# Hybrid decoder step: the first GLA tile's gate behind the sampled chunks, scaling inside their folds, and the mixed rows' loads and high parts in another order

## The chip, the cores and the metric

The kernel runs on one core of a Trainium2 chip. TensorE (PE) multiplies matrices into PSUM banks; VectorE (DVE), ScalarE (ACT) and GpSimd (POOL) work on SBUF and PSUM; SyncE (SP) issues nearly all transfers, one after another. Each engine goes through its own instructions in order, and waits where an operand is not there. The metric is the device time in microseconds of one execution.

## What is computed

One layer of a decoder for 2048 prompt rows and 64 sampled rows (8 sequences of 8), width 1024, in float32:

```python
h = rms_norm(x, g_mix_pre)
proj = jnp.einsum('btd,de->bte', h, w_in)
q, k, v, gq, gk, gv, gr, glr = jnp.split(proj, points, axis=-1)
# group A: sliding-window attention with sinks on q, k, v
# group B: gated linear attention, 4 heads, dk 64, dv 128
log_a = log_sigmoid(glr @ w_gk2 + b_gk) / 16
o, s_new = gla_chunked(gq, gk, gv, log_a, s_init)
o = rms_norm(o, g_gla) * silu(gr)
mix = jnp.concatenate([attn, gla_out], -1) @ w_out
x = x + rms_norm(mix, g_mix_post)
# then x + rms_norm(relu(rms_norm(x) @ w_up) ** 2 @ w_down)
```

Since the norm before the projection is one factor for a row (`rstd`), the kernel projects the unscaled rows and multiplies the result by `rstd` when it leaves PSUM.

## The kernel before

Matrix products run in a TensorE format of fewer bits, so each operand is split into a high and a low part, and three products (high-high, high-low, low-high) make one. The 2048 prompt rows are 16 tiles of 128 rows; the 64 sampled rows are a 17th, number 16 (`NB`).

The program has stages. In the first, attention (group A) runs, and the transposed rows go to DRAM. In the second, which the change touches and which lies at about 305 to 680 us of the profile, the gated linear attention goes through the 16 tiles in order (`gla(i)`, a generator), while TensorE fills the gaps between its small products with projections. This second stream, `fill`, is made by `products`: for the sampled rows, and then for tiles 2 to 15, four chunks of 384 columns each (`projecting`), and after the last chunk the output projection (`out_projecting`) of the first two mixed tiles, 0 and 4. The tables `G_FIRST_FILL`, `G_FILL` and `G_LAST_FILL` say how many products of `fill` TensorE does at each `yield` of `gla(i)`; nothing else sets the order, and ScalarE, VectorE and SP do their parts in the order in which the program is written (`InOrder`, whose line 143 the profile names for nearly all of them).

A chunk's products go into one of two PSUM banks of the kind `a`. A chunk of a prompt tile is copied out by ScalarE, times `rstd`. The sampled rows have 64 rows alone, so their low parts are laid beside the high ones: one product of 128 rows gives both halves. Then `folded` has ScalarE copy the lower 64 rows of the bank to `gp_s` and VectorE add the upper 64, and a second ScalarE copy multiplies by `rstd`. Only after VectorE's addition may TensorE use the bank again, for the chunk after next.

In `gla(i)`: level sums of the log decays of 16 to 64 rows, weighted keys and queries (`XK`, `XQ`), the decays of the next tile, the gate (`gate`: four passes of ScalarE and two products over `sg`), the first level sums of the next tile, the queries and keys of the next tile turned by VectorE (`turn`, through `blocks` and DRAM `qk_d`); then TensorE's level products (`gl`, `gh`, `ds`), VectorE's masked copies of them to `AH`, the copies to `AT`, and, some twenty `fill` products later, the products `o` with `AT`. The steps for the sampled rows (`gla_sample`) lie between those of the tiles from tile 1 on.

At the end of the stage, with tile 15 (the last of `fill`), the weights of a done chunk give their place to the output weights `wo`, which had been split and stored to DRAM before (`wo_d`), and to the mixed rows of tiles 0 and 4:

```python
if after is None:
    load_wo(ks, c)
    if c == G_ORDER[1]:
        placed = [place_mix(j) for j in B_ORDER[:2]]
```

`load_wo` puts `k` = 0 to 2 in the place of chunk 1, 3 to 5 in that of chunk 2, 6 and 7 in that of chunk 3, the first 512 columns first; `place_mix` loads the raw rows to `mt` in the place of chunk 0; `split_mix` with `apart` makes their high parts on ScalarE at once and puts their low parts on the list `lows`, from which `gla(15)` takes them.

Of the kernel before, what the change touches and what calls it, by code (L numbers as in the profile page):

```python
# [16 lines left out]
ALU = mybir.AluOpType  # L17
# [57 lines left out]
G_ORDER = (0, 1, 2, 3)  # L75
G_FILL = (3, 5, 6, 10, 8, 2, 14, 4, 4, 10, 8, 20)
G_LAST_FILL = (2, 4, 5, 7, 6, 2, 11, 2, 3, 7, 6, 15)
G_FIRST_FILL = (6, 6, 6, 10, 10, 4)
S_WAIT = (2, 6)
WO_PARTS = ((), (0, 1, 2), (3, 4, 5), (6, 7))  # L80
B_ORDER = (*(j + b for j in range(4) for b in (0, 4)), NB, *(j + b for j in range(4) for b in (8, 12)))
# [72 lines left out]
def hybrid_step_kernel(ctx: ExitStack, tc: tile.TileContext, I, O):  # L154
# [481 lines left out]
    def projecting(i, xT, chunks, act=nc.scalar):  # L636

        n, waiting = rows(i), []
        for c in chunks:
            p_ = bank([P, 512], "a", f"gproj_{i}_{c}")  # L640
            _, wh, wl = gw[c]
            products = ((xT[1], wh), (xT[1], wl)) if i == NB else ((xT[0], wh), (xT[0], wl), (xT[1], wh))
            for k in range(KT):
                for u, (x, w) in enumerate(products):
                    te.matmul(
                        p_[:, :G_N], x[:, k, :], w[:, k, :],
                        start=k + u == 0, stop=k == KT - 1 and u == len(products) - 1,
                    )
                    yield
                    if waiting and (k, u) == (0, 2):  # L650
                        act.activation(*waiting.pop(), scale=rstd_all[:n, i : i + 1])
            if i not in gps:
                gps[i] = gp_pool.tile([P, G_W], F32, tag="gp", name=f"gp_{i}", bufs=2)
            out = gps[i][:n, c * G_N : (c + 1) * G_N]
            src = folded(out, p_[:, :G_N], act, dv) if i == NB else p_[:, :G_N]
            if act is ac and (i, c) == (0, chunks[0]):
                waiting.append((out, src, AF.Copy))
            else:
                act.activation(out, src, AF.Copy, scale=rstd_all[:n, i : i + 1])
            projected.add((i, c))  # L660

    def load_cache(name, c):
# [408 lines left out]
    s_oT = ss.tile([P, 4, NS], F32, name="s_oT")  # L1071
    s_sg = ss.tile([NS, 512], F32, name="s_sg")
    s_kx = s_work[:NS].rearrange("p (b k) -> p b k", b=DB)
    nc.gpsimd.memset(next(afters), 0.0)
    for u in range(2):
        nc.vector.memset(S[u], 0.0)
# [206 lines left out]
    def gla(i, gp, og=iter(())):  # L1283
# [3 lines left out]
        assert {(i, 0), (i, 1)} <= projected  # L1287
        before, after = pre.pop(i)
        ends = i in (0, NB - 1)
        fills = iter(G_LAST_FILL if i == NB - 1 else G_FILL if i else G_FIRST_FILL + G_FILL[6:])  # L1290
        if ends:
            qkTs_of[i] = next(qkTs)
            qk_T(i, gp, P, "c")
# [44 lines left out]
        weighted_queries(XQ, dec, qz, 6, LEVELS[6], dv)  # L1338
        yield next(fills) + 2 * (i == 1), False
        next(following, None)  # L1340
        sg = next(sgs)
        gating = gate(i, gp, P, sg)
        yield next(fills), True
# [2 lines left out]
        deque(following, 0)  # L1346
        sums = first_sums(*pre[i + 1], dec) if i < NB - 1 else iter(())
        next(sums, None)
        if i + 1 < NB - 1:
            assert {(i + 1, 0), (i + 1, 1)} <= projected  # L1350
            turn(i + 1, gps[i + 1])
        qd = next(qds)
# [43 lines left out]
                        )  # L1396
        for l, gm in enumerate(levels):
            put_level(AH, gm, msk[:, l], LEVELS[l])
        for g in range(2):
            ac.activation(AT[:HD, 2 * g : 2 * g + 2, HD:], far[half_of[g]], AF.Copy)  # L1400
        put[:] = [dv.tensor_copy(AT[half_of[1], :, half_of[1]], AH[half_of[1]])]
# [109 lines left out]
    def split_mix(i, m, ks, raw, apart=False):  # L1511
        n = rows(i)
        if apart:
            hi, lo = m[:, 1], m[:, 2]
            ac.activation(hi, raw, AF.Copy)
            for k in range(0, KT, 4):
                kk = slice(k, k + 4)
                lows.insert(
                    len(lows) if k else len(lows) // 2,
                    lambda kk=kk: dv.tensor_tensor(lo[:, kk], raw[:, kk], f32(hi[:, kk]), op=ALU.subtract),  # L1520
                )
            return [[m[:, u, k, :n] for k in range(ks)] for u in (1, 2)]
        if i == NB:
            split_copy(m[:, 1, :, :NS], m[:, 1, :, NS:], raw[:, :, :NS])
            return m[:, 1], None
        split_copy(m[:, 1, :ks, :n], m[:, 2, :ks, :n], raw[:, :ks, :n])
        parts = [[m[:, u, k, :n] for k in range(ks)] for u in (1, 2)]
        if i == NB - 1:
            for t, late in zip(parts, late_mix):
                t.extend(late[:, h, :] for h in range(4))  # L1530
        return parts
# [76 lines left out]
    def products():  # L1608

        xT = {G_NEXT[0]: first_xT}  # L1610
        for i, after in zip(G_NEXT, (*G_NEXT[1:], None)):
# [6 lines left out]
            for c, ks in zip(G_ORDER, WO_PARTS):  # L1618
# [4 lines left out]
                yield from columns  # L1623
                if after is None:
                    load_wo(ks, c)
                    if c == G_ORDER[1]:
                        placed = [place_mix(j) for j in B_ORDER[:2]]
                    if c == G_ORDER[3]:
                        load_wo_half(range(KT), 1)
                        for h, t in enumerate(g_mix):  # L1630
                            sq.dma_start(t, gain_d[h : h + 1].rearrange("a d -> (a d)").partition_broadcast(P))
                        raw = ss.tile([P, KT, P], F32, tag="part1", name="mt_raw", bufs=2)
                        i = B_ORDER[2]
                        sq.dma_start(raw, mix_d[i])
# [39 lines left out]
    wo, pre, ogs_of, mixes, late_mix, g_mix, put, placing, x1_first = {}, {}, {}, {}, [], [], [], [], []  # L1674
    wo_parts = iter(())
    first_xT = load_T(G_NEXT[0], x_place(G_NEXT[0]), sq)
    early, x_loads, put_off, lows, out_stage = [], [], [], [], []

    def take(waiting, n=None):
        for _ in range(len(waiting) if n is None else min(n, len(waiting))):  # L1680
            waiting.pop(0)()
# [912 lines left out]
```

## Time and profile before

| what | value |
|---|---|
| median of 3 runs | 2158.43 us (2155.21 to 2159.4) |
| profiled execution | 2157.64 us, of which the span of its instructions is 2155.9 us |
| TensorE busy | 2135.3 us, 99% of the span |
| VectorE, ScalarE, GpSimd busy | 1521.8, 1220.1, 242.3 us |
| granted TensorE clock, mean | 0.997 |

A row of the timeline gives the start and the length of an instruction or of some equal ones in us, its engine, line and operation, what it writes and reads, and in brackets how long the engine stood idle before it and what ended that. A row of the windows gives a stretch, its length, the busy time of PE, PEld (weight loads), DVE, ACT and POOL with their instructions, the granted clock as a share of full speed, the share of the DMA engines that were busy, and GB/s. A row of the waits gives who waited for whom: us in total, times, longest. A row of the groups gives the line, the engine, the operation, what it writes and reads, shapes and count, then the busy time and the mean in ns, then the idle time before it and what ended most of it. A row of the chain of waits gives a start, a length and the work. Matmuls overlap: in a merged row of several, the length is from the first start to the last end.

### The profile page before, as it was taken

To read this page: it belongs to the slowest core of one execution; us is meant where nothing else is said; L and a number is where in the kernel's file an instruction comes from. 1 tells how busy PE (TensorE), PEld (TensorE's weight loads), DVE (VectorE), ACT (ScalarE), POOL (GpSimd) and SP (SyncE) were. 2 spreads that over 40 slices of the span, in tenths; PEclk is the share of its full clock that TensorE was granted. 3 is DMA by queue.
4 is the path that set the end of the run, shared out by engine and by line. 5 is a ranking of instruction groups with operands and counts; after the bars stand their busy time and mean duration, and the time that the engine had idled before them with its cause. 6 is when DMAs were issued, how large, how long until landed. Compare 5 with 4: busy or idle time off the path is not lost.

```text
span 2155.9 us, 34631 instructions
## 1 busy us (share of the span) xinstructions
PE 2135.3 (99%) x11888; PEld 1848.5 (86%) x11888; DVE 1521.8 (71%) x3167; ACT 1220.1 (57%) x2694; POOL 242.3 (11%) x407
## 2 busy tenths in 40 slices
PE   9999999999999999999999999999999999999998
PEld 9999998999997888888888887888888888888887
DVE  7999877777785666888887545548776666555576
ACT  7999866566665444655555544445444445544454
POOL 4676510111111110000000000000000000000000
PEclk9999999999999999999999999999999999999999
DMA  7444333455658567778786777668544443766685
GB/s 242 155 144 149 102 101 85 115 130 148 191 171 298 189 219 236 240 249 279 257 277 219 258 249 217 211 198 279 176 171 160 152 156 124 261 202 193 193 272 177
DMA packets 303053, 422.79 MB, mean 196 GB/s; under 512 B 79436, under 2 KB 204860, under 8 KB 298764
## 3 DMA queue, kind: packets, MB, share of 16 engines
q1 hardware_dynamic: 302716, 420.30, 60.3%
q8 instruction: 94, 1.54, 0.3%
q14 instruction: 83, 0.68, 0.1%
q10 hardware_dynamic: 160, 0.27, 0.0%
HBM read 271.39 MB, written 149.62 MB: 195 GB/s over the span
## 4 chain that ended last, share of the span: by engine, by line
PE 86%; DVE 5%; ACT 4%; DMA 3%; issue 1%; SPq 0%; POOL 0%; DVEq 0%; ACTq 0%; POOLq 0%
PE dn L143 26%; PE uX L143 8%; PE gproj L143 8%; PE uc L143 8%; PE out L1556 7%; PE proj L143 6%; PE ue L143 4%; PE ud L143 4%; PE ub L143 4%; PE dsam L143 1%; PE sam L143 1%; PE sc L143 1%; PE pT L143 1%; PE av L143 1%; PE out L143 1%
## 5 line engine op out<-in xcount | busy, mean ns | idle before, releaser
L143 PE MATMUL dn<-o0t,o0s 128*128 128x512 f32 x888 | 345.4, 389 | 0.8 <-ACT f L2335 0.6
L143 PE MATMUL dn<-o0t,o1s 128*128 128x512 f32 x888 | 345.7, 389 | 0.0
L143 PE MATMUL dn<-o1t,o0s 128*128 128x512 f32 x888 | 345.6, 389 | 0.0
L2218 DVE TENSOR_TENSOR o1s<-rs,o0s 128x512 fp32r<-128x512 f32 x224 | 154.4, 690 | 225.1 <-ACT o0s L2217 222.9
L2217 ACT ACTIVATE o0s<-rs 128x512 fp32r<-128x512 f32 x224 | 141.2, 631 | 292.4 <-PE dn L143 263.1
L143 PE MATMUL gproj<-wg,gxh 128*128 128x384 f32 x1024 | 272.3, 343 | 3.9 <-DVE gp_s L143 3.9
L143 ACT ACTIVATE st<-st 128x512 f32<-128x512 f32 x224 | 141.0, 630 | 104.0 <-DVE st L143 99.3
L143 PEld LDWEIGHTS dn<-o0t,o0s 128*128 128x128 f32 x888 | 166.8, 188 | 37.1 <-ACT f L2335 1.0
L143 PEld LDWEIGHTS dn<-o1t,o0s 128*128 128x128 f32 x888 | 166.7, 188 | 35.3
L143 PEld LDWEIGHTS dn<-o0t,o1s 128*128 128x128 f32 x888 | 166.7, 188 | 34.9
L143 PEld LDWEIGHTS gproj<-wg,gxh 128*128 128x128 f32 x1024 | 184.6, 189 | 6.7 <-DVE gp_s L143 4.2
L143 PE MATMUL gproj<-wg,gxl 128*128 128x384 f32 x576 | 187.6, 343 | 1.4 <-DVE gp_s L143 1.4
L143 PE MATMUL uc<-H,s 128*128 128x512 f32 x768 | 186.5, 391 | 1.1 <-ACT st L143 1.1
L143 PE MATMUL uX<-H,w 128*128 128x512 f32 x768 | 185.2, 390 | 0.0
L143 PEld LDWEIGHTS uc<-H,s 128*128 128x128 f32 x768 | 143.0, 188 | 31.6 <-ACT st L143 1.3
L143 PEld LDWEIGHTS uX<-H,w 128*128 128x128 f32 x768 | 144.0, 188 | 30.3
L1556 PE MATMUL out<-wo,mt 128*128 128x512 f32 x680 | 158.6, 392 | 0.0
L2218 DVE TENSOR_TENSOR o1t<-rt,o0t 128x512 fp32r<-128x512 f32 x222 | 151.8, 684 | 4.2 <-ACT o0t L2217 4.1
L1556 PEld LDWEIGHTS out<-wo,mt 128*128 128x128 f32 x680 | 126.5, 188 | 26.2 <-DVE mt L232 0.2
L221 POOL TENSOR_TENSOR frs<-rs_v,half 128x1 f32<-128x1 f32 (+1 forms) x13 | 12.4, 961 | 1199.9 <-DVE rs_v L219 681.3
L2217 ACT ACTIVATE o0t<-rt 128x512 fp32r<-128x512 f32 x222 | 137.2, 619 | 8.0 <-DMA rt<-t_d 4.3
L143 DVE TENSOR_TENSOR st<-st 128x512 f32<-128x512 f32 x160 | 110.6, 691 | 30.6 <-ACT st L143 26.3
(451 smaller groups left out, 4278.7 us busy)
## 6 DMA issues: line engine op xcount, KB each, us to landing
s_d<-st SPq DMA_DIRECT2D x32, 1792.0 KB, 7.6
rs<-s_d SPq DMA_DIRECT2D x224, 256.0 KB, 3.3
raw<-in_w_up SPq DMA_DIRECT2D x64, 512.0 KB, 4.2
rt<-t_d SPq DMA_DIRECT2D x128, 256.0 KB, 3.7
rt<-in_w_down SPq DMA_DIRECT2D x96, 256.0 KB, 2.9
t<-in_w_down SPq DMA_DIRECT2D x64, 256.0 KB, 3.7
t_d<-t SPq DMA_DIRECT2D x32, 512.0 KB, 4.3
h_d<-ht SPq DMA_DIRECT2D x8, 1280.0 KB, 7.6
```

The lines of the kernel that those rows point to most:

```text
L143: ins = call(*a, **k)
L221: return nc.gpsimd.tensor_tensor(out, v[:n], e, op=ALU.pow)
L1556: te.matmul(banks[c], x, w[:, c * 512 : (c + 1) * 512], start=k + u == 0, stop=k == KT - 1 and u == n - 1,)
L2217: high = nc.scalar.activation(hi, raw, AF.Copy)
L2218: low = nc.vector.tensor_tensor(lo, raw, f32(hi), op=ALU.subtract)
```

## The change

Five things are changed.

1. `projecting`, sampled rows: ScalarE's copy of the lower 64 rows multiplies by `rstd` at once, and VectorE's addition becomes a multiply-and-add that scales the upper 64 rows. The second ScalarE copy goes. For the first, `rstd` of the sampled rows has to stand on the lower 64 partitions too: one transfer of 64 x 1 on SP's queue, at the start of the stage's set-up.
2. The fills of tile 0: 22, 4, 4, 5, 5, 20 in place of 14, 4, 4, 10, 8, 20 from the seventh on (the sum of both is 60), so that the steps of tile 0 after its seventh `yield`, the gate among them, are written behind the third sampled chunk.
3. `turn(1)`, which readies tile 1, is written before that `yield` and not after it.
4. The loads of the mixed rows of tiles 0 and 4 are issued after chunk 0 of tile 15 and not after chunk 1.
5. The high parts of these rows are put on a list `highs`, which `gla(14)` takes behind its level copies and ahead of its copies to `AT`.

```diff
-G_FIRST_FILL = (6, 6, 6, 10, 10, 4)
+G_FIRST_FILL = (6, 6, 6, 10, 10, 4, 22, 4, 4, 5, 5, 20)
...
             out = gps[i][:n, c * G_N : (c + 1) * G_N]
-            src = folded(out, p_[:, :G_N], act, dv) if i == NB else p_[:, :G_N]
             if act is ac and (i, c) == (0, chunks[0]):
-                waiting.append((out, src, AF.Copy))
+                waiting.append((out, p_[:, :G_N], AF.Copy))
+            elif i == NB:
+                act.activation(out, p_[NS:, :G_N], AF.Copy, scale=rstd_all[NS:, i : i + 1])
+                dv.scalar_tensor_tensor(out, p_[:NS, :G_N], rstd_all[:n, i : i + 1], out, op0=ALU.mult, op1=ALU.add)
             else:
-                act.activation(out, src, AF.Copy, scale=rstd_all[:n, i : i + 1])
+                act.activation(out, p_[:, :G_N], AF.Copy, scale=rstd_all[:n, i : i + 1])
...
     s_kx = s_work[:NS].rearrange("p (b k) -> p b k", b=DB)
+    sq.dma_start(rstd_all[NS:, NB : NB + 1], rstd_all[:NS, NB : NB + 1])
...
-        fills = iter(G_LAST_FILL if i == NB - 1 else G_FILL if i else G_FIRST_FILL + G_FILL[6:])
+        fills = iter(G_LAST_FILL if i == NB - 1 else G_FILL if i else G_FIRST_FILL)
...
         yield next(fills) + 2 * (i == 1), False
         next(following, None)
+        if i == 0:
+            turn(1, gps[1])
         sg = next(sgs)
         gating = gate(i, gp, P, sg)
         yield next(fills), True
...
         sums = first_sums(*pre[i + 1], dec) if i < NB - 1 else iter(())
         next(sums, None)
-        if i + 1 < NB - 1:
+        if 0 < i < NB - 2:
             assert {(i + 1, 0), (i + 1, 1)} <= projected
             turn(i + 1, gps[i + 1])
...
         for l, gm in enumerate(levels):
             put_level(AH, gm, msk[:, l], LEVELS[l])
+        take(highs)
         for g in range(2):
             ac.activation(AT[:HD, 2 * g : 2 * g + 2, HD:], far[half_of[g]], AF.Copy)
...
         if apart:
             hi, lo = m[:, 1], m[:, 2]
-            ac.activation(hi, raw, AF.Copy)
+            highs.append(lambda: ac.activation(hi, raw, AF.Copy))
...
                 if after is None:
                     load_wo(ks, c)
-                    if c == G_ORDER[1]:
+                    if c == G_ORDER[0]:
                         placed = [place_mix(j) for j in B_ORDER[:2]]
...
-    early, x_loads, put_off, lows, out_stage = [], [], [], [], []
+    early, x_loads, put_off, highs, lows, out_stage = [], [], [], [], [], []
```

TensorE's own order is the same, row for row. First place: ScalarE and VectorE in tile 0, around the second and third sampled chunk (`gproj_1`, `gproj_2`; the numbers after the last underline are buffers). ScalarE before, and then of the change:

```order
L143 ACTIVATE gp_s<-gproj_1_5176 64x384
L143 ACTIVATE gp_s<-gp_s,rstd_all 64x384
L143 ACTIVATE sg_5019<-gp_4479 128x512
L143 ACTIVATE sg_5019<-sg_5019 128x512 x2
L143 ACTIVATE dec_5021<-before_5022 128x128
L143 ACTIVATE dec_5021<-before_5022 128x64x2
L143 ACTIVATE dec_5021<-after_5023 128x64x2
L143 ACTIVATE sg_5019<-sg_5019 128x512
L143 ACTIVATE dec_5021<-before_5022 128x32x4
L143 ACTIVATE dec_5021<-after_5023 128x32x4
L143 ACTIVATE gp_s<-gproj_2_5215 64x384
L143 ACTIVATE gp_s<-gp_s,rstd_all 64x384
```

```order
L143 ACTIVATE gp_s<-gproj_1_5176,rstd_all 64x384
L143 ACTIVATE gp_s<-gproj_2_5223,rstd_all 64x384
L143 ACTIVATE sg_5019<-gp_4479 128x512
L143 ACTIVATE sg_5019<-sg_5019 128x512 x2
L143 ACTIVATE dec_5021<-before_5022 128x128
L143 ACTIVATE dec_5021<-before_5022 128x64x2
L143 ACTIVATE dec_5021<-after_5023 128x64x2
L143 ACTIVATE sg_5019<-sg_5019 128x512
L143 ACTIVATE dec_5021<-before_5022 128x32x4
L143 ACTIVATE dec_5021<-after_5023 128x32x4
L143 ACTIVATE gp_s<-gproj_3_5242,rstd_all 64x384
```

The copy of the third chunk has moved from behind the gate (`sg`) and the next tile's first level sums (`dec`) to right behind the second chunk's, and the scaling copies are gone. VectorE, before and of the change:

```order
L143 TENSOR_TENSOR XQ<-dec_5021,qz 128x256
L143 TENSOR_TENSOR gp_s<-gp_s,gproj_1_5176 64x384
L143 SCALAR_TENSOR_TENSOR before_5022<-z_5202,zt_5030 128x256
L143 TENSOR_TENSOR after_5023<-after_5023,before_5022 128x128
L1221 SCALAR_TENSOR_TENSOR s_oT<-gp_s 64x256
L143 TENSOR_TENSOR before_5022<-before_5022 128x128
L143 STREAM_TRANSPOSE blocks<-gp_4722 128x4x4x32
```

```order
L143 TENSOR_TENSOR XQ<-dec_5021,qz 128x256
L143 STREAM_TRANSPOSE blocks<-gp_4722 128x4x4x32
L143 SCALAR_TENSOR_TENSOR gp_s<-gproj_1_5176,rstd_all,gp_s 64x384
L143 SCALAR_TENSOR_TENSOR gp_s<-gproj_2_5223,rstd_all,gp_s 64x384
L143 SCALAR_TENSOR_TENSOR before_5022<-z_5202,zt_5030 128x256
L1224 SCALAR_TENSOR_TENSOR s_oT<-gp_s 64x256
L143 TENSOR_TENSOR after_5023<-after_5023,before_5022 128x128
L143 TENSOR_TENSOR before_5022<-before_5022 128x128
```

Both folds now stand ahead of the next tile's decays, and the transpose of tile 1 (`blocks`) ahead of both folds. The third fold stood behind all rows shown before, and seven more.

Second place: the end of the stage, SP's queue after the keys of tile 14 (`kd`), before and of the change:

```order
L143 DMA kd_5013<-kd_d_183 128x4x32 x2
L143 DMA wo_1_9244<-wo_d_147 128x512
L143 DMA wo_1_9245<-wo_d_147 128x512
L143 DMA wo_1_9244<-wo_d_148 128x512
L143 DMA wo_1_9245<-wo_d_148 128x512
L143 DMA wo_1_9244<-wo_d_149 128x512
L143 DMA wo_1_9245<-wo_d_149 128x512
L143 DMA mt_9252<-mix_d_63 128x1024
L143 DMA mt_9254<-mix_d_67 128x1024
L143 DMA wo_d_154<-wop_7_9194 128x1024
```

```order
L143 DMA kd_5013<-kd_d_183 128x4x32 x2
L143 DMA mt_9188<-mix_d_63 128x1024
L143 DMA mt_9190<-mix_d_67 128x1024
L143 DMA wo_1_9245<-wo_d_147 128x512
L143 DMA wo_1_9246<-wo_d_147 128x512
L143 DMA wo_1_9245<-wo_d_148 128x512
L143 DMA wo_1_9246<-wo_d_148 128x512
L143 DMA wo_1_9245<-wo_d_149 128x512
L143 DMA wo_1_9246<-wo_d_149 128x512
L143 DMA wo_d_154<-wop_7_9195 128x1024
```

The two `mt` loads have gone past the six `wo` loads. ScalarE in tile 14, before and of the change:

```order
L143 ACTIVATE mo_5016<-ogT_9289 128x512
L143 ACTIVATE mt_9252<-mt_9252 128x1024
L143 ACTIVATE mt_9254<-mt_9254 128x1024
L143 ACTIVATE gp_9187<-gproj_2_9256,rstd_all 128x384
L143 ACTIVATE AT<-gh_9327 64x2x64 x2
L143 ACTIVATE AT<-AH 64x4x64
```

```order
L143 ACTIVATE mo_5016<-ogT_9286 128x512
L143 ACTIVATE gp_9184<-gproj_2_9253,rstd_all 128x384
L143 ACTIVATE mt_9188<-mt_9188 128x1024
L143 ACTIVATE mt_9190<-mt_9190 128x1024
L143 ACTIVATE AT<-gh_9322 64x2x64 x2
L143 ACTIVATE AT<-AH 64x4x64
```

The high parts (`mt`) have changed places with the copy of tile 15's third chunk (`gp`); they stay ahead of the copies to `AT`.

## The prediction

> **What bounds the kernel now.** First the busy table of the page, then TensorE's own waits, then the windows around the two largest, with the granted clock.
>
> ```profile
> PE 2135.3 (99%) x11888; PEld 1848.5 (86%) x11888; DVE 1521.8 (71%) x3167; ACT 1220.1 (57%) x2694; POOL 242.3 (11%) x407
> PE gproj L143 <- DVE gp_s L143: 5.3, 3, 3.9
> PE o L143 <- ACT AT L143: 2.3, 1, 2.3
> ```
>
> TensorE is the bound: 2155.9 - 2135.3 leaves 20.6 us in which it stands still, and only a wait of TensorE, or a slow clock on it, is worth anything. The two largest waits are those that the edits touch: three for a bank of `gproj` that VectorE has not folded (5.3 us), one for `AT` (2.3 us). The second price of a wait shows in the windows (busy time by engine, then the granted clock):
>
> ```profile
> 324.00:327.30 3.30, 2.09 (x12) 1.77 (x11) 1.54 (x4) 2.63 (x6) 0.00 (x0) 1.00 0.25 39
> 330.60:334.00 3.40, 1.41 (x4) 1.41 (x5) 2.14 (x6) 2.00 (x6) 0.00 (x0) 0.51 0.40 76
> 334.00:337.50 3.50, 3.50 (x53) 3.06 (x54) 0.80 (x3) 2.50 (x4) 0.00 (x0) 0.50 0.78 145
> 651.50:655.00 3.50, 3.50 (x12) 2.82 (x11) 2.32 (x7) 2.01 (x8) 0.00 (x0) 0.51 1.00 363
> ```
>
> After each wait the clock stands at half: until 337.5 after the first, from 651.5 to 655 after the second. A wait of 1.21 us at 324.4 left it at 1.00. So a wait that takes over half of some 3.4 us costs itself and then a half-speed stretch. By the Trainium skill (TensorE: Matmul & The Clock Gate, "Why this matters for your kernels") it takes a gap of over about 3 us to lose the clock; here 2.32 us was enough, and by that rule the second wait would have had no second price (1.7 us less in term two's upper bound below), and the second rival would fall away. I go by the rows.
>
> **The folding of the sampled chunks.** The program's time up to here is unchanged, so I rebuild the stretch in absolute time.
>
> ```profile
> 319.63 0.49 ACT L143 ACTIVATE gp_s<-gproj 64x384 f32<-64x384 f32 x1
> 321.34 0.62 ACT L143 ACTIVATE gp_s<-gp_s,rstd_all 64x384 f32<-64x384 f32 x1 [1.23 <-DVE gp_s L143]
> 321.36 3.09 PE L143 MATMUL gproj<-wg,gxl 128*128 128x384 f32 x16 [0.19 <-DVE gp_s L143]
> 321.86 0.30 ACT L143 ACTIVATE dec<-before 128x128 f32<-128x128 f32 x1
> 322.77 0.41 DVE L143 TENSOR_TENSOR XQ<-dec,qz 128x256 f32<-128x256 f32 x1
> 322.91 0.95 SPq L143 DMA_DIRECT2D kd<-kd_d  x2
> 324.54 0.49 ACT L143 ACTIVATE gp_s<-gproj 64x384 f32<-64x384 f32 x1
> 325.06 0.55 DVE L143 TENSOR_TENSOR gp_s<-gp_s,gproj 64x384 f32<-64x384 f32 x1 [1.87 <-ACT gp_s L143]
> 325.66 3.04 PE L143 MATMUL gproj<-wg,gxl 128*128 128x384 f32 x16 [1.21 <-DVE gp_s L143]
> 328.56 0.70 DVE L143 STREAM_TRANSPOSE blocks<-gp 128x512 f32<-128x512 f32 x1
> 331.14 0.47 ACT L143 ACTIVATE gp_s<-gproj 64x384 f32<-64x384 f32 x1
> 332.00 0.54 DVE L143 TENSOR_TENSOR gp_s<-gp_s,gproj 64x384 f32<-64x384 f32 x1
> 332.59 1.01 PE L143 MATMUL gproj<-wg,gxh 128*128 128x384 f32 x2 [3.89 <-DVE gp_s L143]
> 341.85 0.38 PE L143 MATMUL o<-gp,AT 128*128 128x128 f32 x2
> ```
>
> The third fold waits for ScalarE's copy at 331.14, behind tile 0's gate and the first level sums of tile 1, though its chunk ended at 321.36 + 3.09 = 324.45.
>
> *Removed:* four scaling copies of 0.62 us on ScalarE, and its stand of 1.23 us for the first fold. The fold with a scale, VectorE's scalar-and-tensor form, is not in the trace at this size; its nearest rows are the folds it replaces, 0.55 us with the same two operands, and I take that (half or double moves no wait by over 0.5 us). ScalarE's scale now rides in the copy: 0.49 us as before.
>
> *First chunk:* its fold stands where it stood, so 0.19 us stays. *Second:* ScalarE runs on at 320.1 instead of 321.86, so the second copy ends 1.74 us before 325.03, at 323.3. VectorE is free at 323.2, but the transpose of tile 1 now stands ahead of the fold: 0.70 us, to 323.9. It overwrites `blocks`, which the stores to `kd_d` read; the `kd` loads at 322.91 wait for the same stores, so it waits for nothing more. The fold ends at 324.4. TensorE, done with issuing the third chunk at 321.36 + 16 x 0.18 = 324.2 (0.18 from (3.04 - 0.34)/15), waits 0.2 us, not 1.21. *Third:* copy 324.5 to 325.0, fold to 325.55; the fourth chunk runs from 324.4 to 327.3, so the bank is free in time and the 3.89 us are gone. *Fourth:* its copy comes after the gate, near 330, its fold near 331; its bank is wanted only 26 `gproj` products on.
>
> TensorE then goes 327.3; six products of tile 2, 1.1 us; the level products, for which I take a warm tile:
>
> ```profile
> 405.16 1.08 PE gl L143 x32
> 406.24 0.69 PE gh L143 x20
> 406.93 0.44 PE ds L143 x8
> ```
>
> 2.2 us, to 330.6; twenty products, 3.6 us, to 334.2, where `o` asks for `AT`. Before, that was at 341.85: **7.6 us** earlier, of which 4.9 us are waits (1.0 and 3.9), 2.4 us the half clock (from 332.6 to 337.5) and the rest the pipe running empty.
>
> *What is late next:* `AT`. The level copies on VectorE now follow the fourth fold, and `s_sg` stands between them and the copy to `AT`:
>
> ```profile
> L143 DVE COPY_PREDICATED AH<-c,gl 128x128 f32<-128x128 uint8 x4 | 1.4, 362 | 2.8 <-PE gl L143 2.7
> L1116 DVE SCALAR_TENSOR_TENSOR s_sg<-gp_s,s_sg 64x512 f32<-64x512 f32 x1 | 0.7, 704 | 0.0
> 343.94 0.29 DVE L143 TENSOR_TENSOR after<-after,before 128x128 f32<-128x128 f32 x1 [2.72 <-ACT dec L143]
> ```
>
> From 331.0, six level copies (2.3 us), `s_sg` (0.7) and the `AT` copy (0.3) end at 334.3; ScalarE's two `AT` parts end about then. I book 0.1 us, and up to 1 us as a bound. What is left of the sampled gate, one more product of 0.7 us, falls into the 2.72 us in which VectorE waits for ScalarE at the start of tile 1 (the last row). The added load of the scales, 64 x 1, goes out some 60 us earlier on SP, ahead of loads that wait for TensorE there: nothing. **Term one: 7.5 us**, bounds 3 (second fold a further 2 us late, which brings the half clock back) and 8.
>
> **The mix loads and their high parts.**
>
> ```profile
> 642.49 0.58 ACT L143 ACTIVATE mo<-ogT 128x512 f32<-128x512 f32 x1
> 645.90 1.06 ACT L143 ACTIVATE mt<-mt 128x1024 fp32r<-128x1024 f32 x1 [2.83 <-DMA mt<-mix_d]
> 647.95 1.06 ACT L143 ACTIVATE mt<-mt 128x1024 fp32r<-128x1024 f32 x1 [0.99 <-DMA mt<-mix_d]
> 649.82 0.40 ACT L143 ACTIVATE AT<-AH 64x256 f32<-64x256 f32 x1
> 650.27 0.49 PE L143 MATMUL o<-gp,AT 128*128 128x128 f32 x2 [2.32 <-ACT AT L143]
> 655.59 6.06 PE L143 MATMUL out<-wo,mt 128*128 128x512 f32 x26
> 636.58 2.81 SPq L143 DMA_DIRECT2D wo<-wo_d  x6
> 639.44 1.15 SPq L143 DMA_DIRECT2D mt<-mix_d  x2
> 643.50 21.87 SPq L143 DMA_DIRECT2D wo<-wo_d  x26
> ```
>
> On SP the two `mt` loads change places with six `wo` loads: they go out at 636.58 instead of 639.44, and nothing is ahead of them but `kd`. They then land well before 643.6, when ScalarE has done `mo` and the copy of tile 15's third chunk. The high parts run to 645.8, the `AT` parts follow VectorE's level copies and end near 647.1, and TensorE asks at 647.8. The 2.3 us wait is gone; with the half clock (3.4 us of it, 1.7 lost) that would be 2.47 + 1.7 = 4.1 us.
>
> *What is late next:* the `wo` loads. `out` would now begin 1.48 us behind `o` as before, at 649.3 instead of 651.75, and run through its `k` at 0.227 us a product ((6.06 - 0.39)/25). The queue has eight transfers out at a time, so each issue shows that the one eight places ahead has landed:
>
> ```profile
> SPq L143 <- DMA wo<-wo_d: 9.0, 25, 0.9
> 652.28 1.12 SPq L143 DMA_DIRECT2D wo<-wo_d  x2
> 654.32 0.32 SPq L143 DMA_DIRECT2D wo<-wo_d  x1
> 658.98 0.32 SPq L143 DMA_DIRECT2D wo<-wo_d  x1
> ```
>
> Counted so, the high part of `k` = 3 is there by 652.8, its low part by 654.3, `k` = 7 by 659.0 to 659.7, one each 0.67 us between. The change only reorders what stands before them (the same 2.5 MB), on DMA engines that are full (share 1.00 and over in the windows above), so I leave these landings where they are. TensorE needs `k` = 3 as its 13th and 14th product: before at about 656.1, now at 649.3 + 12 x 0.227 = 652.0. It waits some 0.7 and then 1.4 us, then goes at the pace of the loads, and does the 37th product, the low part of `k` = 7, at about 660.0 where before it did it at 661.5. **Term two: 1.5 us**; bounds 0 (these waits cost the clock again) and 4.1 (the loads come earlier too). I take the end nearer to the landings.
>
> Sum: 7.5 + 1.5 = 9.0 us against the profiled execution's 2157.64 us, of which 2155.9 is the span: 2148.6 us. The median of the runs shown is 2158.43, 0.8 us above; between the two bases I say **2149**.
>
> **The rivals.**
>
> *The loads keep up* (4.1 us in term two): 2157.6 - 11.6 = 2146. For it: the two transfers of `wo_d` go out later. Against it: the full DMA engines.
>
> *The clock drops again in the new wait for `wo`*: two waits of 2.1 us in all within some 3.4 us, just past half, and whether they fall into one stretch is chance. Half speed for 3.4 us costs the 1.5 us: 2150.1.
>
> *The second fold stays late*: the transpose ahead of it, or ScalarE's copy, 2 us behind my times; the third and fourth chunks meet a wait of over 2 us and 2.4 us of half clock: 7.5 - 4.4 = 3.1 in term one, 2153.0. Against it: both predecessors have rows.
>
> *The wait only moves to `AT`*, so that term one does nothing like what its name says: VectorE's order for tile 0 is nearly the same work, and if the fourth fold came at 338 instead of 331, `o` would stand till the old 341.85: about 2156. Against it: VectorE idles 2.7 us for `gl` before its level copies.
>
> *Slower*: the transpose now heads VectorE's queue ahead of two folds, and waits for four stores to land in DRAM. Each us by which they land after 323.1 holds the fold, the bank and TensorE. The gain of 9.0 is gone when they are 6.6 us late (6.6 + 2.4 for the clock), and from 11 us on the kernel is slower by over 0.2%: 2162 at 11. Against it: `kd` at 322.91 shows them landed.
>
> **How the numbers follow.** Chances: the forecast 0.50, loads keep up 0.10, clock drops again 0.20, second fold late 0.12, wait moves to `AT` 0.05, slower 0.03. No change is within 0.2%, 4.3 us, about what a measurement of this kernel can tell. Faster by more: the first three and half of the fourth, 0.86; within: the other half and the fifth, 0.11; slower 0.03. The range runs from the loads that keep up, less 1.5 us for the spread of the runs, 2144.5, to the late second fold plus 1 us, 2154. The forecast alone spans 2147 to 2151.
>
> **What would show it.** The waits for `gp_s` shrink to about 0.4 us in two pieces, and the granted clock is 1.00 throughout 320 to 345. `o` of tile 0 starts near 334.3. The wait of `o` for `AT` in tile 14 is gone, the `mt` copies run without a DMA wait, and TensorE has a new wait within the first forty `out` products, near 645 on the shifted clock, released by `wo`. Wrong would be: a wait over 1 us for `gp_s` or for `AT` in tile 0, a half-clock stretch there, or `out` running without a wait.

## The result, and the profile after

| | before | changed |
|---|---|---|
| median of 5 runs each, us | 2157.50 (2155.21 to 2159.40) | 2146.51 (2144.46 to 2149.40) |
| ratio to before, 95% interval | | 0.9950 (0.9935 to 0.9965) |
| profiled execution, us | 2157.64, span 2155.9 | 2144.46, span 2142.7 |

The changed kernel is faster by 11.0 us of medians; the forecast was 9. In a second series of five its median was 2147.39 against 2157.16, ratio 0.9956 (0.9944 to 0.9969), 9.8 us. First the busy table of the changed kernel's page, then the two of TensorE's waits that lie at the edited places.

```profile
PE 2130.5 (99%) x11888; PEld 1844.3 (86%) x11888; DVE 1522.4 (71%) x3167; ACT 1217.3 (57%) x2690; POOL 242.2 (11%) x407
PE out L143 <- DMA wo<-wo_d: 0.9, 3, 0.6
PE gproj L143 <- DVE gp_s L143: 0.3, 1, 0.3
```

TensorE is still the bound. The 5.3 us of waits for `gp_s` are down to 0.3, and `AT` is gone from the list; the new name is `wo`. The timeline of the changed kernel at tile 0 (start and length in us):

```profile
320.44 6.04 PE L143 MATMUL gproj<-wg,gxl 128*128 128x384 f32 x32 [0.26 <-DVE gp_s L143]
321.94 0.58 ACT L143 ACTIVATE gp_s<-gproj,rstd_all 64x384 f32<-64x384 f32 x1
322.19 0.70 DVE L143 STREAM_TRANSPOSE blocks<-gp 128x512 f32<-128x512 f32 x1
322.82 0.57 DVE L143 SCALAR_TENSOR_TENSOR gp_s<-gproj,rstd_all,gp_s 64x384 f32<-64x384 f32 x1
324.19 0.61 DVE L143 SCALAR_TENSOR_TENSOR gp_s<-gproj,rstd_all,gp_s 64x384 f32<-64x384 f32 x1 [0.80 <-ACT gp_s L143]
329.44 0.60 DVE L143 SCALAR_TENSOR_TENSOR gp_s<-gproj,rstd_all,gp_s 64x384 f32<-64x384 f32 x1
333.22 0.61 DVE L143 SCALAR_TENSOR_TENSOR S<-S,dec,ds 128x128 f32<-128x128 f32 x2
333.33 0.46 PE L143 MATMUL o<-gp,AT 128*128 128x128 f32 x2
333.88 0.30 PEld L143 LDWEIGHTS ds<-gp,AT 128*128 128x128 f32 x2 [0.28 <-DVE S L143]
333.88 0.49 PE L143 MATMUL ds<-gp,AT 128*128 128x128 f32 x2
```

The third and fourth sampled chunks run as one row of 32 products with no wait that the list shows (0.2 us between them is found below), and the third fold follows the second at once. And at the end of tile 14, TensorE's `out` products with what they waited for, and ScalarE's and SP's rows ahead of them:

```profile
628.52 0.92 SPq L143 DMA_DIRECT2D mt<-mix_d  x2
629.48 3.26 SPq L143 DMA_DIRECT2D wo<-wo_d  x6
635.37 2.00 ACT L143 ACTIVATE mt<-mt 128x1024 fp32r<-128x1024 f32 x2
638.76 0.40 ACT L143 ACTIVATE AT<-AH 64x256 f32<-64x256 f32 x1
640.84 3.01 PE L143 MATMUL out<-wo,mt 128*128 128x512 f32 x12
644.42 0.50 PE L143 MATMUL out<-wo,mt 128*128 128x512 f32 x1 [0.57 <-DMA wo<-wo_d]
645.09 1.19 PE L143 MATMUL out<-wo,mt 128*128 128x512 f32 x4 [0.17 <-DMA wo<-wo_d]
646.43 4.87 PE L143 MATMUL out<-wo,mt 128*128 128x512 f32 x20 [0.15 <-DMA wo<-wo_d]
```

The high parts of `mt` wait for no DMA, and after exactly twelve `out` products TensorE stands for the 13th: `k` = 3 of `wo`.

**Where the time went.** In all kernels of this study TensorE does the same 11,888 products in the same order, so two profiles can be laid side by side product by product. "Place one" is how much a kernel gains on the profile of before between the product that starts at 318.1 us there (in the first sampled chunks) and the one at 342.5 (the end of tile 0's `AT` products); "place two" is the same from 600.0 to 664.0 (tiles 13 and 14, `AT`, the first `out` products); "later" is from 664.0 to TensorE's last product. All in us.

| kernel | ahead at 318 | place one | place two | later | ratio of medians to before (95%) |
|---|---|---|---|---|---|
| changed | 1.0 | 7.1 | 2.4 | 2.0 | 0.9950 (0.9935 to 0.9965) |
| changed, second series | 0.5 | 7.2 | 1.8 | -0.2 | 0.9956 (0.9944 to 0.9969) |
| folds only | 1.2 | 5.8 | 0.3 | 1.8 | 0.9962 (0.9948 to 0.9975) |
| mix only | 1.4 | 0.7 | 0.6 | 0.4 | 0.9986 (0.9977 to 0.9995) |
| scaled folds only | 0.7 | 3.3 | -1.3 | 1.5 | 0.9983 (0.9974 to 0.9992) |
| order of tile 0 only | 1.5 | 4.6 | -1.0 | 0.5 | 0.9979 (0.9970 to 0.9988) |
| high parts back | 1.2 | 7.1 | 1.8 | 1.5 | 0.9952 (0.9939 to 0.9964) |
| mix loads back | 0.5 | 7.2 | -2.8 | 1.4 | 0.9965 (0.9952 to 0.9977) |
| no last store | -1.4 | 7.2 | 3.6 | 2.1 | 0.9952 (0.9939 to 0.9964) |
| last part early | 0.7 | 5.8 | 2.3 | 1.6 | 0.9956 (0.9942 to 0.9969) |
| transpose behind | 0.6 | 7.2 | 2.1 | 1.4 | 0.9954 (0.9941 to 0.9968) |
| last part behind the mix | 1.6 | 6.1 | 2.0 | 1.0 | 0.9952 (0.9939 to 0.9964) |
| both | -1.9 | 7.2 | 2.1 | 1.2 | 0.9953 (0.9940 to 0.9965) |

The profiles of before and changed differ by 13.2 us of span, but only 7.1 + 0.1 + 2.4 = 9.6 us of that lie at the two places and between them. The 1.0 us ahead of tile 0, the 2.0 behind the stage and 0.6 behind the last product lie where nothing was edited. The first two differ as much between the kernels of the table (from -1.9 to 1.6, and from -0.2 to 2.1) and are taken for the chance of single executions; "later" is above zero in all rows but one, so the profile of before may be a slow one there. The 0.6 is not chance: from the last product to the end it is 7.1 to 7.2 us in the three kernels without the scaled folds and 6.5 to 6.7 in all eleven profiles with them. These kernels have one transfer more on SP's queue, so every later transfer signals another of the eight semaphores that the queue goes through in turn; the last store is done 2.1 us behind its issue in the changed kernel and 2.5 in before. Whether the one brings the other was not tried. Place one and place two are what the experiments are read by; the medians carry 2 to 3 us of uncertainty each way.

### The profile page after: what moved, and what is told of

The parts are those of the page before. It is cut to its first block, busy times and chain, and to the rows that moved or that the text cites. A ratio compares the mean times of both kernels' runs of the same rounds, so it can differ in the third digit from the quotient of the medians.

```text
span 2142.7 us, 34628 instructions
## 1 busy us (share of the span) xinstructions
PE 2130.5 (99%) x11888; PEld 1844.3 (86%) x11888; DVE 1522.4 (71%) x3167; ACT 1217.3 (57%) x2690; POOL 242.2 (11%) x407
## 4 chain that ended last, share of the span: by engine, by line
PE 88%; DVE 5%; ACT 3%; DMA 2%; issue 1%; POOL 0%; SPq 0%; DVEq 0%; ACTq 0%; POOLq 0%
PE dn L143 28%; PE uc L143 8%; PE uX L143 8%; PE gproj L143 8%; PE out L1562 7%; PE proj L143 6%; PE ue L143 4%; PE ud L143 4%; PE ub L143 4%; PE dsam L143 1%; PE sam L143 1%; PE sc L143 1%; PE pT L143 1%; PE av L143 1%; PE out L143 1%
```

## The two parts alone

Edits: the kernel before with the parts 1 to 3 of the change alone (folds, fills, `turn`), and with the parts 4 and 5 alone (mix loads, high parts). The diffs are the hunks shown above.

> The kernel before with the first part alone (scaled folds, the fills of tile 0, the transpose of tile 1 ahead of the gate, the load of the scales); the mix loads and high parts as before. If the parts are independent, as the forecast has it: 7.5 us less than before, ratio 0.9965, of which TensorE's waits for the folded banks give 4.9 and the half clock behind them 2.4; the wait of 2.3 us for AT in tile 14 and its half clock stay as they were. Rival: the first part only wins what the second one keeps (the late AT wait of tile 14 grows when tile 0 ends earlier): under 5 us.

> The kernel before with the second part alone (mix loads a chunk earlier, high parts beside the levels). The forecast: 1.5 us less than before (ratio 0.9993), with waits of about 2.1 us for wo in place of the one for AT. What the two profiles show when their products are laid side by side: 2.5 us less (0.9988), with 0.9 us of waits. Rival (loads keep up): 4.1 us less and no wait for wo. In each case the waits for the folds stay at 5.3 us.

Measured: folds only 2148.59 us against 2156.12 of before, a gain of 7.5 us of medians; mix only 2153.63, a gain of 2.5. So both parts gain, and their sum, 10.0, lies between the 9.8 and 11.0 of the whole. But the profiles show that neither gain is one fixed number. TensorE's waits, folds only and then mix only:

```profile
PE o L143 <- ACT AT L143: 2.9, 1, 2.9
PE gproj L143 <- DVE gp_s L143: 2.0, 2, 1.8
```

```profile
PE gproj L143 <- DVE gp_s L143: 5.3, 3, 3.8
PE out L143 <- DMA wo<-wo_d: 1.5, 2, 1.4
```

With the folds alone, a wait of 1.8 us for the second fold is back, and place one is 5.8 and not 7.1: the third rival of the prediction, of which more below. The wait for `AT` is 2.9 us there, and yet place two gains 0.3, because this time the clock stays up. With the mix alone, the wait for `wo` is longer than in the changed kernel, and this time the clock drops (second rival). The windows of the granted clock, folds only around its `AT` wait, and mix only around its `wo` wait (length, busy time of PE, PEld, DVE, ACT, POOL, then the clock):

```profile
638.95:642.37 3.42, 2.11 (x12) 1.78 (x11) 1.22 (x5) 1.82 (x2) 0.00 (x0) 1.00 1.04 390
642.37:645.78 3.41, 1.84 (x14) 1.79 (x15) 0.21 (x1) 1.50 (x5) 0.00 (x0) 1.00 1.03 321
```

```profile
648.50:651.91 3.41, 1.88 (x8) 1.02 (x7) 3.09 (x10) 2.08 (x12) 0.00 (x0) 1.00 1.03 375
651.91:655.32 3.41, 3.41 (x9) 2.63 (x10) 2.92 (x11) 3.07 (x14) 1.08 (x1) 0.50 1.04 384
```

One wait of 2.9 us, cut by the border of two windows into 1.3 and 1.6 us of idle time, cost only itself; waits of 1.5 us that fell into one window cost a half-speed stretch on top, and left 0.6 us of the second part's gain.

## Which half of the first part carries it

Edits: the kernel before with the scaled folds and the load of the scales alone; and with the fills and the place of `turn(1)` alone, each fold still copied, added, scaled.

> The kernel before with the scaled folds alone: fills of tile 0 and the transpose where they stood. Theory (the place of tile 0's gate carries the gain, the shorter fold only the 1.2 us of the second one): the second wait of 1.21 us goes to about 0, the third fold still stands behind the gate and the first level sums, so its wait stays between 3 and 4 us and the half clock with it: 0.5 to 1.5 us less than before. Rival (ScalarE's scaling copies and its stand for VectorE carry it): both waits go and 5 to 7 us are gained.

> The kernel before with the new order of tile 0 alone (fills and transpose), each fold still copied, added and then scaled. Theory: the third fold follows the second at once, its wait of 3.9 us shrinks below 1.5 and the half clock goes; the second fold, now behind the transpose as well as behind the scaling copy, is late by 1.2 to 2 us: 4 to 6 us less than before. Rival (the scaling carries it): waits of over 2 us and a half-clock stretch stay, under 2 us less.

Measured: 2152.65 and 2151.33 us against 2156.12, gains of 3.5 and 4.8; at place one 3.3 and 4.6. The first expectation missed: the scaling is worth more than twice the most that the theory gave it, though not what its rival said. TensorE's waits at the folds with the scaling alone:

```profile
320.71 5.82 PE L143 MATMUL gproj<-wg,gxl 128*128 128x384 f32 x32 [0.21 <-DVE gp_s L143]
329.33 0.61 PE L143 MATMUL gproj<-wg,gxh 128*128 128x384 f32 x2 [2.80 <-DVE gp_s L143]
```

The second fold's wait of 1.21 us is gone, as said, but the third shrank as well, from 3.89 to 2.80 us: the third fold is done 2.5 us sooner (329.33 + 0.7, by which the two profiles differ at 318 us, against 332.59), while TensorE asks 1.5 us sooner. The 2.5 us fit what ScalarE no longer has ahead of that fold, two scaling copies of 0.62 and a stand of 1.23 us. And only one window of half clock is left of two. With the order alone the third wait is gone, and two waits are left: 1.24 us for the second fold, and a new one for `AT`, whose cause ScalarE's timeline shows:

```profile
332.13 0.62 ACT L143 ACTIVATE gp_s<-gp_s,rstd_all 64x384 f32<-64x384 f32 x1 [0.95 <-DVE gp_s L143]
332.78 0.63 ACT L1112 ACTIVATE s_sg<-gp_s 64x512 f32<-64x512 f32 x1
...
334.76 0.56 ACT L143 ACTIVATE AT<-gh 64x128 f32<-64x128 f32 x2
335.22 0.40 ACT L143 ACTIVATE AT<-AH 64x256 f32<-64x256 f32 x1
```

TensorE's row for `o`, next, starts when that copy has ended:

```profile
335.68 0.49 PE L143 MATMUL o<-gp,AT 128*128 128x128 f32 x2 [1.53 <-DVE blocks L143]
```

The fourth fold's stand and scaling copy hold ScalarE until 332.78; the three passes of `s_sg`, then `AT`, come behind. (The wait is put down to VectorE's `blocks`, but ScalarE's copy to `AT` ended last, at 335.62.) So the two halves work at different waits: the scaling at the second fold and at ScalarE's queue ahead of `AT`, the order at the third fold. Alone they gain 3.3 + 4.6 = 7.9, together 7.1.

## Which half of the second part carries it

Edits: the changed kernel with one of its two parts undone.

```diff
-            highs.append(lambda: ac.activation(hi, raw, AF.Copy))
+            ac.activation(hi, raw, AF.Copy)
```

> The changed kernel with the high parts back where they were made before (ahead of ScalarE's copy of tile 15's third chunk instead of behind it); the mix loads stay a chunk earlier. Theory (the loads carry the second part): ScalarE's two copies run without a wait for DMA, there is no wait for AT, and the time is that of the changed kernel within 0.5 us (ratio to before 0.995 to 0.996). Rival (the place of the high parts carries it): the wait for AT comes back with over 1 us, 2 to 4 us more than the changed kernel.

```diff
-                    if c == G_ORDER[0]:
+                    if c == G_ORDER[1]:
                         placed = [place_mix(j) for j in B_ORDER[:2]]
```

> The changed kernel with the mix loads back behind the six wo loads; the high parts stay beside the levels. Theory (the loads carry it): ScalarE waits 3 to 4.5 us for the mix loads again, the AT copies stand behind, TensorE waits 2.3 to 3.4 us for AT, and no wait for wo is left: 0.5 to 4 us more than the changed kernel, by whether that wait falls into one stretch of the clock or is cut by two. Rival: the place of the high parts alone removes the wait for AT, and the time is that of the changed kernel within 0.5 us.

Measured: with the high parts back 2145.97 us, place two 1.8, inside what the changed kernel shows itself (1.8 and 2.4); with the loads back 2150.10, place two -2.8. The loads carry the part; the place of the high parts moves nothing that can be seen. ScalarE's row for the first high part, and TensorE's for `o`, with the loads back:

```profile
640.65 1.06 ACT L143 ACTIVATE mt<-mt 128x1024 fp32r<-128x1024 f32 x1 [4.69 <-DMA mt<-mix_d]
644.12 0.80 PE L143 MATMUL o<-gp,AT 128*128 128x128 f32 x2 [3.72 <-ACT AT L143]
```

In before these two waits were 2.83 and 2.32 us; in the four other profiles with the loads at their old place TensorE's was 2.9 to 3.7. By this wait the profile of before was the mildest of the five, so what the second part removes can be more than the forecast could read from it: between this run and the changed kernel's, place two differs by 2.4 + 2.8 = 5.2 us. That is the largest difference, not the usual one. The mean of place two is -1.0 over the five profiles with the loads at their old place, and 1.7 over the five with the loads a chunk earlier and all stores where they were: 2.7 us, close to the 2.5 us of medians of mix only.

## What limits the second part: the loads of wo

Edits: the changed kernel without the two stores of the last block (`k` = 7) of the split output weights; and with all work done, but that block split and stored a tile earlier, once ahead of tile 12's mix and once behind it.

```diff
         def keep_parts(k, parts):
-            for u in range(2):
+            for u in range(2 if k < KT - 1 else 0):
                 sq.dma_start(wo_d[k][:, u], f32(parts[u]))
...
-                sq.dma_start(f32(wo[k][u][:, cc]), wo_d[k][:, u, cc])
+                sq.dma_start(f32(wo[k][u][:, cc]), wo_d[min(k, KT - 2)][:, u, cc])
```

> The changed kernel without the two stores of the last block (k = 7) of w_out's parts to DRAM, 1 MB of traffic that stands between the mix loads and the load of k = 3; the out product takes the parts of k = 6 a second time in its place, so this step of the computation is left out. Theory (after the change TensorE's out products go at the pace of the DMA engines, 0.67 us for 256 KB, so 2.7 us less of them ahead): k = 3 lands 1.5 to 2.7 us earlier, the three waits for wo (0.9 us) and the slow pace behind them go, 1.0 to 1.7 us less than the changed kernel. Rival (the loads start when tile 15's weights come free, and what stands ahead of them does not matter): waits for wo and time as in the changed kernel.

```diff
+        if i == NB - 3:
+            next(wo_parts, None)
         take(put_off)
         yield next(fills), False
         deque(og, 0)
```

> The changed kernel with the last block (k = 7) of w_out split and stored one tile earlier, in tile 13 directly behind that of k = 6: all work done, the 1 MB of stores out of the way of the wo loads. Theory (pace of the DMA engines): as without these stores, waits for wo gone, 1.0 to 1.7 us less than the changed kernel, unless ScalarE's and VectorE's further copy (about 1.1 us each) in tile 13 makes TensorE wait there (rival: a new wait of 0.5 to 1.1 us in tile 13, which gives the gain back).

```diff
         deque(og, 0)
+        if i == NB - 3:
+            next(wo_parts, None)
+            take(put_off)
         yield next(fills), True
```

> The changed kernel with the last block of w_out split and stored in tile 13 again, but behind the mix of tile 12 (which TensorE waited 1.2 us for when the split stood ahead of it) and ahead of the level products. Theory: no wait for wo, no wait for mo over 0.3 us, the second part's gain rises from 2.4 to the 3.6 us seen without the stores: 1.2 us less than the changed kernel. Rival: the split delays VectorE's level copies of tile 13 and with them AT there, a wait of 0.5 to 1.5 us that takes the gain back.

Without the stores no wait for `wo` is left, and place two is 3.6 us, 1.2 to 1.8 more than in the changed kernel: what stands ahead of the loads of `wo` on the DMA engines is what makes `out` wait. TensorE's rows there:

```profile
643.37 5.28 PE L143 MATMUL out<-wo,mt 128*128 128x512 f32 x22
648.85 3.70 PE L143 MATMUL out<-wo,mt 128*128 128x512 f32 x15 [0.21 <-DVE mt L143]
```

Twenty-two products run through, where the changed kernel stood at the 13th. In the trace's record the first part of `k` = 3 lands 3.0 us sooner there than in the changed kernel, both counted from the product at 600.0 us. Beside before, this kernel is 4.2 us ahead from the 12th product to the 22nd (counted from 600.0 us), while the changed kernel has 4.1 at the 12th and 2.4 at the 37th. The median, 2145.88, is 0.6 to 1.5 us below the changed kernel's two, a difference that the medians cannot tell from none; the profile is what shows it.

Both versions that do all the work removed the wait for `wo` as well (that part lands 1.8 and 1.6 us sooner than in the changed kernel), and paid for it in tile 13. TensorE's row with the block ahead of the mix, and then VectorE's rows and TensorE's with the block behind it:

```profile
617.26 0.32 PE L143 MATMUL o<-S,qd 64*64 64x128 f32 x1 [1.25 <-ACT mo L143]
```

```profile
615.87 1.28 DVE L143 SCALAR_TENSOR_TENSOR wop<-wor,ggla,wop 128x1024 fp32r<-128x1024 f32 x1
617.07 1.58 DVE L143 COPY_PREDICATED AH<-c,gl 128x128 f32<-128x128 uint8 x4
...
619.74 0.60 DVE L143 SCALAR_TENSOR_TENSOR S<-S,dec,ds 128x128 f32<-128x128 f32 x2
620.39 0.49 PE L143 MATMUL o<-gp,AT 128*128 128x128 f32 x2 [1.21 <-DVE S L143]
```

The split takes 1.1 us of ScalarE and 1.3 us of VectorE, and at both spots that engine is already what TensorE waits for next. At the 12th `out` product the lead on before is 2.8 and 2.6 us, where it is 4.1 in the changed kernel, so tile 13 costs 1.3 to 1.5 us. Place two is 2.3 and 2.0, and the medians, 2146.82 and 2146.11, are the changed kernel's. In both expectations the rival came true.

## When the second fold is late

In the changed kernel VectorE's transpose of tile 1 stands ahead of the second fold. It writes `blocks`, which the four stores to `kd_d` read. The prediction took these stores to be done in time, from SP's `kd` loads of one profile. The folds-only run shows them late; SP's, VectorE's and TensorE's rows:

```profile
318.65 1.77 SPq L143 DMA_DIRECT2D kd_d<-blocks  x4
323.88 0.94 SPq L143 DMA_DIRECT2D kd<-kd_d  x2
323.85 0.71 DVE L143 STREAM_TRANSPOSE blocks<-gp 128x512 f32<-128x512 f32 x1 [1.78 <-DMA kd_d<-blocks]
325.11 3.04 PE L143 MATMUL gproj<-wg,gxl 128*128 128x384 f32 x16 [1.78 <-DVE gp_s L143]
```

Over the profiles of all 13 kernels (before among them) and the changed kernel's second one, the time from the first of these stores to the `kd` loads, which wait for them, is of two kinds: 3.1 to 3.3 us in nine, 4.8 to 5.2 us in five. Among the eight that have scaled folds and the transpose ahead, three are of the late kind (folds only, last part early, last part behind the mix), and place one is 5.8, 5.8 and 6.1 there, where it is 7.1 to 7.2 in the other five: about 1.3 us. The edit that takes the cause away moves the transpose behind the third fold:

```diff
-        if i == 0:
-            turn(1, gps[1])
         sg = next(sgs)
         gating = gate(i, gp, P, sg)
         yield next(fills), True
+        if i == 0:
+            turn(1, gps[1])
```

> The changed kernel once more, beside the three below. Ratio to before 0.995 to 0.996, as measured. In its profile either no wait for the second fold (VectorE's transpose of tile 1 starts at about 322.2 us), or, as in two of the six profiles with the new order so far, one of about 1.7 us, because that transpose waits for the stores to kd_d; the wait for wo about 1 us in sum.

> The changed kernel with the transpose of tile 1 behind the second and third folds instead of ahead of them. Theory (the transpose's wait for the kd_d stores is the only thing that makes the second fold late): the folds never wait for a DMA, TensorE's waits for gp_s are 0.3 us whenever those stores land, and the time is that of the changed kernel or up to 0.6 us less (1.7 us in a third of the executions). Rival (tile 1's queries and keys then arrive late, since their stores go out 2 to 3 us later): a new wait of TensorE or VectorE for qkT in tile 1, 1 to 3 us more.

> Both edits (transpose behind the folds, last block of w_out behind the mix of tile 12). Theory: the two are independent, 1.2 to 1.8 us less than the changed kernel, ratio to before 0.9945 to 0.995, with no wait for gp_s over 0.3 us, none for wo, and the clock at full speed throughout. Rival: one of the new waits named for them alone shows, and the time is that of the changed kernel or more.

Measured: 2147.39, 2146.41 and 2145.82 us (ratios 0.9956, 0.9954, 0.9953): alike. In the kernel with both edits the stores were late, and the folds did not care; its SP, VectorE and TensorE rows:

```profile
321.68 1.92 SPq L143 DMA_DIRECT2D kd_d<-blocks  x4
326.85 0.93 SPq L143 DMA_DIRECT2D kd<-kd_d  x2
325.39 0.61 DVE L143 SCALAR_TENSOR_TENSOR gp_s<-gproj,rstd_all,gp_s 64x384 f32<-64x384 f32 x1 [0.29 <-ACT gp_s L143]
323.28 5.82 PE L143 MATMUL gproj<-wg,gxl 128*128 128x384 f32 x32 [0.26 <-DVE gp_s L143]
```

The second fold starts 1.5 us before the stores are done, and place one is the full 7.2. No wait for `qkT` of tile 1 appeared in either run, so that rival fell. What is left is small: 1.3 us in three profiles of eight, 0.5 us on average, below what these series tell apart. "Both" did not come to 1.2 to 1.8 us less, since the block of `wo` gives its share back in tile 13. No version here is shown to beat the changed kernel.

## Why the prediction was right, and where it was off

*Sum and time.* 9.0 us were forecast, 9.6 are found at the two places, 11.0 and 9.8 in two series of medians. The time lies inside the range, 0.5 us under the span that was given for the forecast alone. That the sum fits better than its terms is luck: term one was 0.4 too high, term two 0.3 to 0.9 too low.

*Folds, step by step.* Shifted by the 1.0 us by which the two profiles differ already at 318 us, the second fold ends at 323.39 + 1.0 = 324.4 as forecast, and the first `o` product starts at 333.33 + 1.0 = 334.3, as forecast. The 0.2 us wait for that fold came as well, too short for the list: the products of the next chunk begin at 323.44, right behind the fold, and the row of 32 takes 6.04 us, where it takes 5.82 in two runs whose second fold is in time (scaled folds only, and "both"). The drag of `AT`, booked at 0.1, came so; another 0.3 us that the sum did not have is behind it, at `ds`: its pair starts 0.55 us behind `o` and not 0.22 as before, when VectorE's update of `S`, which reads `ds`, has ended at 333.22 + 0.61. Term one is 7.1 where 7.5 was forecast. The added load of the scales was put at nothing, and no wait in this stage comes of it; the 0.6 us at the end of the program go with the kernels that have it. The two rows that were taken for others were near: the scaled fold takes 0.57 to 0.61 us against 0.55, ScalarE's scaled copy 0.58 against 0.49; no wait in TensorE's list comes of either. The clock stays at 1.00, and the three waits of 5.3 us are one of 0.3 in the list and the 0.2 beside it, the 0.4 in two pieces of the forecast.

*The step that was unsafe* is "so it waits for nothing more". It holds in five of eight profiles with the scaled folds and that order; in three the transpose waits for the `kd_d` stores. It is the third rival with nearly the lateness that it was priced for (1.4 to 1.8 against 2 us) but with no half clock behind it, so 1.3 us and not 4.4; and it is the mechanism of the "slower" rival at a small size: the stores were late by 2 us, never by 6.6.

*Mix.* The chain is as written: the wait for `AT` gone, no DMA wait ahead of the high parts, a new wait at the 13th product, released by `wo`. Counted from 600.0 us, the changed kernel is 4.1 us ahead of before at the 12th product, the whole upper bound of term two, and 2.4 at the 37th: the three waits for `wo`, 0.9 us in the list, and the emptied pipe behind each take 1.8 back. From the 18th product on TensorE goes at its own 0.23 us a product and waits no more; the loads, one each 0.67 us, stay just ahead of it.

Term two is mis-sized, 1.8 to 2.4 against 1.5, and the step is "I leave these landings where they are". The landings of before were read rightly: in the trace's record of landings the two parts of `k` = 3 are complete at 652.61 and 654.30. In the changed kernel they are complete at 644.38 and 645.04. This kernel is 8.2 us ahead at 600.0, so on the clock of before that is 652.6 and 653.3: the first part lands when it did, the second 1.0 us sooner, and so do all loads behind it up to `k` = 7. In the changed kernel's second profile the low part of `k` = 7 lands 0.4 us sooner. With 1.0 and 0.4 us the forecast's own sum gives 2.5 and 1.9, where 2.4 and 1.8 were found. In before the last of the sixteen pieces of that second part came 1.0 us behind the fifteenth; no run shows why.

*Rivals.* "The clock drops again in the new wait" was seen once in five profiles that have that wait (mix only), with 0.6 us left of the term, near the 0 of the forecast's bound. "The loads keep up" came without the stores, and in the three versions with the last block earlier ("both" among them), which lost nearly as much in tile 13. "The wait only moves to `AT`" is what the order without the scaling does, with 1.5 us.

## What to carry to other kernels

A wait that ends at one time in one profile may end 2 us later in the next execution: before an edit puts work behind a DMA that "has landed by then", look at how much later it may land, and put the work that the bounding engine waits for ahead of it. When a load is moved forward, the next load in the same queue is what stands next; count from which product on it is needed. And lay two profiles side by side by the bounding engine's instructions: that tells a place's gain to 0.1 to 0.6 us (the changed kernel's two profiles), where medians tell 2 to 3 us, and separates it from what differs elsewhere.

## What the runs showed of the clock

Between the first microseconds and the last twenty of these profiles, every half-clock stretch is one or two windows of 3.41 us long, and within a profile they start a whole number of 3.41 us apart (in before the first starts 324.27 us behind the start of full speed, 95 windows, and the second 320.85 us later, 94); from run to run the grid lies elsewhere. What counts is the idle time inside one window of that grid, not the length of the wait. The windows of before around its `AT` wait, and of the kernel with the mix loads back around its own:

```profile
648.09:651.50 3.41, 1.23 (x11) 1.23 (x12) 0.00 (x0) 2.12 (x5) 0.00 (x0) 1.00 1.05 296
651.50:654.91 3.41, 3.41 (x12) 2.73 (x11) 2.23 (x7) 2.01 (x8) 0.00 (x0) 0.50 1.00 363
```

```profile
639.85:643.26 3.41, 0.55 (x4) 0.22 (x2) 0.00 (x0) 2.06 (x3) 0.00 (x0) 1.00 1.04 334
643.26:646.67 3.41, 2.55 (x12) 2.56 (x13) 0.00 (x0) 0.79 (x4) 0.00 (x0) 0.50 1.03 362
646.67:650.08 3.41, 3.41 (x10) 2.73 (x9) 2.45 (x7) 2.01 (x8) 0.00 (x0) 0.50 1.03 375
```

A window in which TensorE is busy for 1.23 or 0.55 us is followed by one at half speed; and one at half speed with 2.55 us busy (a quarter idle) is followed by another, which a quarter of idle time at full speed never was. Idle shares of 57% and more always dropped the clock, shares up to 38% never; between them the share alone does not decide, since 46% kept it twice (folds only), 47 and 53% kept it near the end of the program (last part early; changed, second series), and 45% lost it (mix only). What else counts there stays open; the prediction's "over half of some 3.4 us" comes near, but is met by the 53% that kept the clock and not by the 45% that lost it. The Trainium skill (TensorE: Matmul & The Clock Gate, "Part 1: The HAM clock gate (the "warmup" mystery)") gives a free-running window of 3413 ns, and the length and the grid here agree; by its table half speed follows at least one idle window, and here windows with 1.23 and 1.88 us of work in them were enough.

So the price of a wait between about 1.5 and 3.4 us depends on where the grid happens to lie: in the five profiles with a wait of 2.3 to 3.7 us for `AT` in tile 14, four lost the clock behind it and one, with 2.9, did not. This and the two kinds of landing of the `kd_d` stores, whose cause was not tried, may be part of what makes executions of one kernel differ by some us; no run here shows how much.
